# The end of a hybrid retention, state-space and expert block: early operands, a merged order for the two token blocks, and transposes spawned later

## The chip, the cores and the metric

One NeuronCore of one Trainium2 chip runs the whole program, in one launch. The metric is device time in microseconds (us). TensorE (PE) does the matrix products, VectorE (DVE), ScalarE (ACT) and GpSimd (POOL) the elementwise work; SyncE (SP) issues nearly all DMAs, and ACT a few of the stores.

## The reference, cut to what matters

One layer on 256 tokens and 16 meta tokens, model width 2048, all in float32. The parts that the change touches are the last lines of each stage:

```
merged = sigmoid(gate_ret) * y_ret + sigmoid(gate_ssm) * y_ssm
h = h + merged @ w_out                       # residual
xn = rmsnorm(h, norm_ffn_g)
# peer_ffn, here for all 128*128 experts with a sparse gate matrix:
#   u = gelu(xn @ exp_u.T);  Z = gate * u;  y = Z @ exp_v
h = h + y
return rmsnorm(h, norm_final_g)[:, N_META:]  # 256 x 2048
```

## The kernel before, in words

All weights stream from HBM once, as pieces of 128x512. SP loads two pieces at a time (`raw`, 128x1024, four buffers). Each piece is split into a high part `wh` (ACT, L99) and a rest `wl` (DVE, L100), four buffers of each, and TensorE multiplies in three passes: high times high, high times low, low times high.

The order of all work is set by one class, `Stream`. Its `run` goes through the queue of pieces; `now` is the piece's number. For each piece it first splits the piece two places ahead (`self.split(self.now + self.LEAD)`, which also issues the load of the piece six places ahead of that), then calls the piece's hook if it has one, then runs the side work that is due (`due()`), and last the piece's own matmuls. Side work is made of Python generators: `st.spawn(gen, delay, urgent)` puts one on a heap to be resumed `delay` pieces later, and a `yield 1` inside it puts off its next step by one piece. Nothing of this happens on the chip; it only fixes the order in which instructions stand in each engine's queue. Each engine then works through its queue in order and waits on semaphores.

**The merge.** `mixer_out` is called twice; the second call (weights `wso`, `wgs`) makes the merged activations in four column blocks `j` of 512. Products of the kind `product_tok` have the tokens on the partitions: weights are the moving operand, and the matmuls of two pieces are issued together at the odd one, 6 for token block b=0, 6 for b=1 (L234 to L236). When the last piece of a column block is done, `done(b, p)` forms gate times product (DVE, L442), one piece later adds it to `Q.mt` (DVE, L444), and for b=1 spawns `turn(Q.mt, j, merged)`. `turn` transposes the column block in two groups of four 128x128 transposes on TensorE (L463), one piece for ACT to take the result (L469), one for DVE to take the rest (L471), then the second group. `Q.nmerged` counts the finished rows, and the next product (`wout`) asks for them by that count.

**The residual.** The four `wout` products end in `resid(j)`: DVE adds the product to `Q.h2` (L795), and for b=1 a `turn(Q.h2, j, scaled)` is spawned, whose parts are read by the query products `wq` (L206 to L208, 12 matmuls for one piece); the residual is also stored to HBM, to `Q.h2d`.

**The last stage.** Z lies in two tiles: `Q.za`, the first 88 units, on the left side of the on-chip memory, and `Q.zb`, the last 40, on the right. In the V stage, unit `i` of 128 takes four pieces of 128x512; `split_w(i)` makes the high and low part of Z's row block `i` (pool `wp`, two buffers, on the right) two units ahead, and the matmuls (L1063 to L1065) add into eight PSUM tiles `Q.y[q, b]`, column quarter q and token block b. For the last unit the matmuls wait for all four pieces and then run b=0 with q=0..3, and b=1 with q=0..3. `fin_open`, hooked to piece 2 of the last unit, gives back `wp` and `zbp` and opens the pool `fin` in their place; into it SP loads the residual (`Q.h3`, 2 MB, one DMA) and the final norm's weights, spread over the partitions (`Q.gfin`, 1 MB, one DMA). `finish(b)` is called once for each token block: four adds from PSUM on DVE (L1100), four squares with a row sum on ACT (L1101), four products with the weights on POOL (L1102), the sum and the reciprocal root (L1103, then `rsqrt`: DVE L162 and a power on POOL, L163), four scalings on DVE (L1107) and four stores, from SP and ACT in turn (L1108).

Of the kernel before, what the change touches and what calls it, by code (L numbers as in the profile page):

```python
# [8 lines left out]
F32 = mybir.dt.float32  # L9
F32R = mybir.dt.float32r  # L10
U32 = mybir.dt.uint32
AF = mybir.ActivationFunctionType
OP = mybir.AluOpType
AX = mybir.AxisListType
# [3 lines left out]
D = 2048  # L18
# [4 lines left out]
EPS = 1e-6  # L23
# [3 lines left out]
NE = 128  # L27
ZB = 40
# [98 lines left out]
def build(ctx, tc, a):  # L127
    nc = tc.nc
    act, vec, pool, pe = nc.scalar, nc.vector, nc.gpsimd, nc.tensor
# [4 lines left out]
    def opened(name, bufs=1, **kw):  # L134
        g = tc.tile_pool(name=name, bufs=bufs, reuse_waits="tile", **kw)
        setattr(P, name, g.__enter__())
        guards[name] = g
        return getattr(P, name)

    def closed(*names):  # L140
        for n in names:
            guards.pop(n).__exit__(None, None, None)
            delattr(P, n)
# [6 lines left out]
    st = Stream(nc, P.raw, P.part)  # L150
# [7 lines left out]
    Q = Names()  # L158

    def rsqrt(dst, ps, mul, add):  # L160

        vec.tensor_scalar(dst, ps, mul, add, op0=OP.mult, op1=OP.add)  # L162
        pool.tensor_tensor(dst, dst, mhalf.to_broadcast(list(dst.shape)), op=OP.pow)  # L163
# [13 lines left out]
    def rows(dst, c, diag):  # L177

        pool.tensor_tensor(diag.rearrange("p (b t) -> p b t", b=2), ident.unsqueeze(1).to_broadcast([128, 2, 128]),
                           c.unsqueeze(2).to_broadcast([128, 2, 128]), op=OP.mult)  # L180
        yield 3
        pe.matmul(dst, ones, diag, start=True, stop=True)
        yield 1
# [61 lines left out]
    def w_in(done, full, hook=None, early=False):  # L245
        i = wcount[0]
        wcount[0] += 1
        c = slice(0 if full else NM, T)
        if early:
            moving, count = lambda: (Q.x0h[:, :, c], Q.x0l[:, :, c]), None  # L250
        else:
            moving, count = lambda: (Q.xh[:, :, c], Q.xl[:, :, c]), lambda: Q.nx
        product([a["win"][i, 0], a["win"][i, 1]], moving, done, hook, count)
# [168 lines left out]
    def mixer_out(name, gate_name, first, hooks):  # L422

        G = {}

        def gate(j):
            def done(b, p):
                if b == 0:
                    G[j] = P.mwork.tile([128, 2, 512], F32, name="sig")
                act.activation(G[j][:, b], p, AF.Tanh, scale=0.5)  # L430
                return
                yield
            product_tok([a[gate_name][j, i] for i in range(8)], lambda: (Q.xh[:, :, NM:], Q.xl[:, :, NM:]), done,
                        hooks.get(("gate", j)))

        def out(j):
            def done(b, p):
                m, t = Q.mt[:, b, j * 512:j * 512 + 512], G[j][:, b]
                if first:
                    vec.scalar_tensor_tensor(m, t, 1.0, p, op0=OP.add, op1=OP.mult)  # L440
                    return
                vec.scalar_tensor_tensor(t, t, 1.0, p, op0=OP.add, op1=OP.mult)  # L442
                yield 1, 0.7
                vec.tensor_add(m, m, t)  # L444
                if b:
                    st.spawn(turn(Q.mt, j, merged), 1, True)
            product_tok([a[name][j, i] for i in range(16)], lambda: (Q.gh, Q.gl), done, hooks.get(("out", j)),
                        lambda: Q.ngated)

        for j in range(4):  # L450
            gate(j)
            out(j)
            if first and j == 1:
                w_in(dt_done, True)

    def turn(x, j, done):

        for i in range(2):
            f = 4 * j + 2 * i
            ps = P.psm.tile([128, 512], F32, name="mix")  # L460
            for n in range(4):
                c = (f + n // 2) * 128
                pe.transpose(ps[:, n * 128:n * 128 + 128], x[:, n % 2, c:c + 128], ident)  # L463
            yield 1
            yield from done(f, ps)
# [324 lines left out]
    def resid(j):  # L790
        c = slice(j * 512, j * 512 + 512)

        def done(b, p):
            h = Q.h2[:, b, c]
            vec.scalar_tensor_tensor(h, p, 0.5, h, op0=OP.mult, op1=OP.add)  # L795
            if b:
                st.spawn(turn(Q.h2, j, scaled), 1, True)
                if j == 3:
                    st.spawn(norm(), 2, True)
                st.spawn(keep_h2(), 8)  # L800
            yield 1, 0, 0.6
            act.activation(P.h2p.tile([128, 512], F32, name="junk"), h, AF.Square, accum_out=Q.ss[:, b, j:j + 1])

        def keep_h2():
            nc.sync.dma_start(Q.h2d[:, :, c], Q.h2[:, :, c])
            return
            yield

        return done
# [10 lines left out]
    def norm():  # L820
        yield 6
        sq = P.bconst.tile([128, 2], F32, name="sq")
        vec.tensor_reduce(sq, Q.ss, axis=AX.X, op=OP.add)
        Q.rt = P.bconst.tile([128, 2], F32, name="rt")
        rsqrt(Q.rt, sq, 1.0 / D, EPS)
        yield 3
        ps = P.psm.tile([128, 512], F32, name="mix")
        yield from rows(ps[:, :S], Q.rt, P.h2p.tile([128, 512], F32, name="junk")[:, :S])
        act.activation(Q.rb, ps[:, :S], AF.Copy)
        st.spawn(topk(), 1)  # L830
# [236 lines left out]
    def vpiece(i, q):  # L1067
        def f(h, lo):
            if i < NE - 1:
                for b in range(2):  # L1070
                    v_mm(i, q, b, h, lo)
                if q == 3:
                    del Q.w[i]
                    if i + 2 < NE:
                        st.spawn(split_w(i + 2), 0)
            else:
                Q.last.append((h, lo))
                if q == 3:
                    for b in range(2):
                        for qq in range(4):  # L1080
                            v_mm(i, qq, b, *Q.last[qq])
                        finish(b)
        return f

    def fin_open():
        closed("wp", "zbp")
        w = opened("fin", side="right")
        Q.h3 = w.tile([128, 2, 4, 512], F32, name="h3")
        nc.sync.dma_start(Q.h3, Q.h2d.rearrange("p b (q f) -> p b q f", q=4))
        Q.gfin = w.tile([128, 4, 512], F32, name="gfin")  # L1090
        nc.sync.dma_start(Q.gfin, bass.AP(tensor=a["gfin"].tensor, offset=a["gfin"].offset,
                                          ap=[[0, 128], [512, 4], [1, 512]]))

    def finish(b):
        w = P.fin
        pp = w.tile([128, 6], F32, name="pp", bufs=2)
        y = w.tile([128, 4, 512], F32, name="y", bufs=2)
        for q in range(4):
            h = Q.h3[:, b, q]
            vec.tensor_add(y[:, q], Q.y[q, b], h)  # L1100
            act.activation(w.tile([128, 512], F32, name="junk"), y[:, q], AF.Square, accum_out=pp[:, q:q + 1])  # L1101
            pool.tensor_mul(h, y[:, q], Q.gfin[:, q])  # L1102
        vec.tensor_reduce(pp[:, 4:5], pp[:, :4], axis=AX.X, op=OP.add)  # L1103
        rsqrt(pp[:, 5:6], pp[:, 4:5], 1.0 / D, EPS)
        for q in range(4):
            h = Q.h3[:, b, q]
            vec.tensor_scalar(h, h, pp[:, 5:6], None, op0=OP.mult)  # L1107
            (act if q % 2 else nc.sync).dma_start(a["out"][b * 128:b * 128 + 128, q * 512:q * 512 + 512], h)  # L1108


    def ret_open():
# [21 lines left out]
    for j in range(2 * PH):  # L1133
        product([a["wq"][j, 0], a["wq"][j, 1]], lambda: (Q.xgh, Q.xgl), query(j), query_open if j == 1 else None,
                lambda: Q.nxg)
        if j == 1:

            q = st.queue[-8:]
# [2 lines left out]
        product([a["pu"][i, 0], a["pu"][i, 1]], lambda: (Q.xgh, Q.xgl), unit(i), u_open if i == 0 else None)  # L1141
    for i in range(NE):
        for q in range(4):
            hook = {(0, 0): v_open, (0, 3): v_open3, (NE - 1, 2): fin_open}.get((i, q))
            st.queue.append((a["pv"][i, q // 2], vpiece(i, q), hook))

    xnp = opened("xn")
# [5 lines left out]
    w = P.ret  # L1153
# [17 lines left out]
    def square(k):  # L1171
        i = 1 if k % 2 else k % 4
        first = k < 3
        sq = acc[:, i] if first else w.tile([128, T], F32, name="t1") if i == 1 else \
            w.tile([128, T], F32, name="xnf", bufs=3)
        if i == 1:
            pool.tensor_mul(sq, ht[:, k], ht[:, k])
        else:
            act.activation(sq, ht[:, k], AF.Square)
        if not first:  # L1180
            (pool if i == 1 else vec).tensor_add(acc[:, i], acc[:, i], sq)
# [154 lines left out]
```

## Time and profile before

| what | value |
|---|---|
| median of 3 runs (lowest to highest) | 3411.99 us (3411.63 to 3413.03) |
| the profiled execution's own time | 3412.41 us |
| its span, first to last instruction | 3410.5 us |
| mean granted TensorE clock | 0.995 of full speed |
| busy in the span: PE / DVE / ACT / POOL | 3358.5 / 2343.0 / 1738.2 / 648.9 us |
| DMA, mean over the span | 182 GB/s |

The time is measured around the program, so that it is 1.9 us above the span. TensorE is at work for almost the whole span; what another engine does costs time only where TensorE waits for it, or after TensorE's last matmul.

### The profile page before, as it was taken

What the parts mean: (1) busy time and instruction counts of PE and PEld (TensorE: products, weight loads), DVE (VectorE), ACT (ScalarE), POOL (GpSimd) and SP (SyncE); (2) the same over time, 40 slices, a digit from 0 to 9 for tenths busy, and PEclk for the clock granted to TensorE, in tenths of its full rate; (3) what the DMA queues carried; (4) which work ended last, traced back from release to release, by engine and by line L of the source; (5) the groups of instructions that cost most, each with busy time, mean ns of one, the idle gap of its engine ahead of it and who ended that gap; (6) DMA issues with size and microseconds to landing.
All of it is one profiled execution on the core that took longest, in us unless ns stands there. A gap on an engine that the chain in (4) does not pass through costs nothing. (4 is left out here: it accounts for less than half of the span.)

```text
span 3410.5 us, 60879 instructions
## 1 busy us (share of the span) xinstructions
PE 3358.5 (98%) x22616; PEld 3103.3 (91%) x22616; DVE 2343.0 (69%) x4518; ACT 1738.2 (51%) x3132; POOL 648.9 (19%) x743
## 2 busy tenths in 40 slices
PE   9999999999999999999999999999999999999996
PEld 8999999888899999977778999999999988888885
DVE  7555555555578878855556899899999655555554
ACT  5444444444455555544455555555555555555553
POOL 2100110000023223310000111356778100000001
PEclk9999999999999999999999999999999999999998
DMA  5555555566655565555566566555555666666664
GB/s 187 163 167 167 167 167 163 174 197 204 188 175 171 179 189 174 173 173 182 181 206 209 175 188 188 180 175 175 178 175 174 190 193 192 195 193 193 195 193 160
DMA packets 172664, 619.80 MB, mean 182 GB/s; under 512 B 20144, under 2 KB 22064, under 8 KB 171856
## 3 DMA queue, kind: packets, MB, share of 16 engines
q1 hardware_dynamic: 168144, 602.15, 57.4%
q0 software_dynamic: 3648, 12.72, 1.3%
q8 instruction: 178, 2.92, 0.4%
q14 instruction: 118, 0.97, 0.1%
q10 hardware_dynamic: 576, 1.05, 0.1%
HBM read 611.52 MB, written 4.33 MB: 181 GB/s over the span
## 5 line engine op out<-in xcount | busy, mean ns | idle before, releaser
L100 DVE TENSOR_TENSOR wl<-raw,wh 128x512 fp32r<-128x512 f32 x2244 | 1633.9, 732 | 995.4 <-ACT wh L99 776.9
L99 ACT ACTIVATE wh<-raw 128x512 fp32r<-128x512 f32 x2244 | 1409.8, 630 | 1320.0 <-PE acc L207 672.5
L206 PE MATMUL acc<-xh,wh 128*128 128x272 f32 (+1 forms) x2704 | 786.8, 291 | 0.0
L208 PE MATMUL acc<-xh,wl 128*128 128x272 f32 (+1 forms) x2704 | 772.0, 286 | 0.6 <-DVE wl L100 0.6
L207 PE MATMUL acc<-xl,wh 128*128 128x272 f32 (+1 forms) x2704 | 769.7, 285 | 0.0
L208 PE MATMUL acc<-xgh,wl 128*128 128x256 f32 x2304 | 644.8, 280 | 0.0
L206 PE MATMUL acc<-xgh,wh 128*128 128x256 f32 x2304 | 644.3, 280 | 0.0
L207 PE MATMUL acc<-xgl,wh 128*128 128x256 f32 x2304 | 644.2, 280 | 0.0
L206 PEld LDWEIGHTS acc<-xh,wh 128*128 128x128 f32 x2704 | 509.9, 189 | 3.9 <-ACT cth L572 1.2
L207 PEld LDWEIGHTS acc<-xl,wh 128*128 128x128 f32 x2704 | 510.0, 189 | 0.7
L208 PEld LDWEIGHTS acc<-xh,wl 128*128 128x128 f32 x2704 | 509.9, 189 | 0.8 <-DVE wl L100 0.8
L207 PEld LDWEIGHTS acc<-xgl,wh 128*128 128x128 f32 x2304 | 433.2, 188 | 0.0
L206 PEld LDWEIGHTS acc<-xgh,wh 128*128 128x128 f32 x2304 | 432.7, 188 | 0.0
L208 PEld LDWEIGHTS acc<-xgh,wl 128*128 128x128 f32 x2304 | 432.6, 188 | 0.0
L1063 PE MATMUL y<-wh,wzh 128*128 128x512 f32 x1024 | 398.7, 389 | 0.0
L1065 PE MATMUL y<-wh,wzl 128*128 128x512 f32 x1024 | 398.6, 389 | 0.0
L1064 PE MATMUL y<-wl,wzh 128*128 128x512 f32 x1024 | 398.6, 389 | 0.0
L1065 PEld LDWEIGHTS y<-wh,wzl 128*128 128x128 f32 x1024 | 192.3, 188 | 39.9
L1064 PEld LDWEIGHTS y<-wl,wzh 128*128 128x128 f32 x1024 | 192.3, 188 | 39.8
L1063 PEld LDWEIGHTS y<-wh,wzh 128*128 128x128 f32 x1024 | 192.3, 188 | 39.7
L979 POOL TENSOR_SCALAR o<-iota,tp 128x128 fp32r<-128x128 f32 x256 | 220.9, 871 | 22.5 <-PE g L995 18.4
L234 PE MATMUL acc<-wh,gh 128*128 128x512 f32 x512 | 199.8, 390 | 0.0
(315 smaller groups left out, 3764.6 us busy)
## 6 DMA issues: line engine op xcount, KB each, us to landing
raw<-in_win SPq DMA_DIRECT2D x354, 512.0 KB, 3.7
raw<-in_pu SPq DMA_DIRECT2D x256, 512.0 KB, 3.6
raw<-in_pv SPq DMA_DIRECT2D x256, 512.0 KB, 3.6
raw<-in_wro SPq DMA_DIRECT2D x64, 512.0 KB, 4.3
raw<-in_wso SPq DMA_DIRECT2D x64, 512.0 KB, 3.9
raw<-in_wga SPq DMA_DIRECT2D x32, 512.0 KB, 3.7
raw<-in_wgs SPq DMA_DIRECT2D x32, 512.0 KB, 3.6
raw<-in_wout SPq DMA_DIRECT2D x32, 512.0 KB, 4.2
```

The source lines that it names most:

```text
L99: self.nc.scalar.activation(h, r, AF.Copy)
L100: self.nc.vector.tensor_sub(lo, r, h.bitcast(F32))
L206: pe.matmul(p, h[:, s], mh[:, kk], start=kk == 0, stop=False)
L207: pe.matmul(p, h[:, s], ml[:, kk], start=False, stop=False)
L208: pe.matmul(p, lo[:, s], mh[:, kk], start=False, stop=kk == nk - 1)
L234: pe.matmul(p, sh[:, k, t], wh, start=k == 0, stop=False)
L979: pool.tensor_scalar(o[:, 0], Q.iota, Q.i1[:, tt], None, op0=OP.is_equal)
L1063: pe.matmul(y, wh[:, s], h, start=i == 0, stop=False)
L1064: pe.matmul(y, wh[:, s], lo, start=False, stop=False)
L1065: pe.matmul(y, wl[:, s], h, start=False, stop=i == NE - 1)
```

## The change: what it does

Three edits. First, in the merge `turn(Q.mt, j, merged)` is spawned with delay 3 instead of 1. Second, in the residual `turn(Q.h2, j, scaled)` is spawned with delay 2 instead of 1. Third, the last stage: `fin_open` is hooked to the first piece of unit 91 (`NE - ZB + 3`) instead of the last unit's third, gives back `zap` (the left part of Z, whose 88 units are used up by then) instead of `wp` and `zbp`, and opens `fin` there. The loads of residual and weights are cut into eight and four DMAs of 256 KB, one every four pieces. `finish` is called once, after all 24 matmuls of the last unit, and writes the instructions of both token blocks in one order; quarters 0 and 1 go by POOL (times the weights) and ACT (times the row's scale, stored from ACT's queue), quarters 2 and 3 in one DVE instruction with both factors (stored from SP's queue).

```
-                    st.spawn(turn(Q.mt, j, merged), 1, True)
+                    st.spawn(turn(Q.mt, j, merged), 3, True)
...
-                st.spawn(turn(Q.h2, j, scaled), 1, True)
+                st.spawn(turn(Q.h2, j, scaled), 2, True)
...
                         for qq in range(4):
                             v_mm(i, qq, b, *Q.last[qq])
-                        finish(b)
+                    finish()
...
     def fin_open():
-        closed("wp", "zbp")
-        w = opened("fin", side="right")
+        closed("zap")
+        w = opened("fin")
         Q.h3 = w.tile([128, 2, 4, 512], F32, name="h3")
-        nc.sync.dma_start(Q.h3, Q.h2d.rearrange("p b (q f) -> p b q f", q=4))
         Q.gfin = w.tile([128, 4, 512], F32, name="gfin")
-        nc.sync.dma_start(Q.gfin, bass.AP(tensor=a["gfin"].tensor, offset=a["gfin"].offset,
-                                          ap=[[0, 128], [512, 4], [1, 512]]))
+        def fetch():
+            h = Q.h2d.rearrange("p b (q f) -> p b q f", q=4)
+            for b in range(2):
+                for q in range(4):
+                    nc.sync.dma_start(Q.h3[:, b, q], h[:, b, q])
+                    yield 4
+            for q in range(4):
+                nc.sync.dma_start(Q.gfin[:, q], bass.AP(tensor=a["gfin"].tensor, offset=a["gfin"].offset + 512 * q,
+                                                        ap=[[0, 128], [1, 512]]))
+                yield 4
+        st.spawn(fetch(), 4)
...
+        def add(b, q):
+            vec.tensor_add(y[:, b, q], Q.y[q, b], Q.h3[:, b, q])
+        def square(b, q):
+            act.activation(w.tile([128, 512], F32, name="junk"), y[:, b, q], AF.Square, accum_out=pp[:, b, q:q + 1])
+        def gain(b, q):
+            pool.tensor_mul(z[:, b, q], y[:, b, q], Q.gfin[:, q])
+        def norm(b):
+            vec.tensor_reduce(pp[:, b, 4:5], pp[:, b, :4], axis=AX.X, op=OP.add)
+            rsqrt(pp[:, b, 5:6], pp[:, b, 4:5], 1.0 / D, EPS)
+        def store(b, q):
+            (act if q < 2 else nc.sync).dma_start(a["out"][b * 128:b * 128 + 128, q * 512:q * 512 + 512], z[:, b, q])
+        def by_act(b, q):
+            act.activation(z[:, b, q], z[:, b, q], AF.Copy, scale=pp[:, b, 5:6])
+            store(b, q)
+        def by_vec(b, q):
+            vec.scalar_tensor_tensor(z[:, b, q], y[:, b, q], pp[:, b, 5:6], Q.gfin[:, q], op0=OP.mult, op1=OP.mult)
+            store(b, q)
         for q in range(4):
+            add(0, q)
+            square(0, q)
+            if q < 2:
+                gain(0, q)
+        norm(0)
         for q in range(4):
+            add(1, q)
+            square(1, q)
+            if q < 2:
+                gain(1, q)
+                by_act(0, q)
+        by_vec(0, 2)
+        norm(1)
+        by_vec(0, 3)
+        for q in (0, 1):
+            by_act(1, q)
+        for q in (2, 3):
+            by_vec(1, q)
...
-            hook = {(0, 0): v_open, (0, 3): v_open3, (NE - 1, 2): fin_open}.get((i, q))
+            hook = {(0, 0): v_open, (0, 3): v_open3, (NE - ZB + 3, 0): fin_open}.get((i, q))
```

The program decides where these instructions stand. On TensorE, at the end of the first column block of the merge: the rows ahead are the last matmuls of the `wso` product (moving weights, `gh` and `gl` the mixer's output), `mix` with `m_90` is the first group of transposes of `Q.mt`, and `acc` with `xh` is the next product.

```order
 L235 MATMUL acc<-wh,gl 128x512
 L236 MATMUL acc<-wl,gh 128x512
+L234 MATMUL acc<-wh,xh 128x512
+L235 MATMUL acc<-wh,xl 128x512
+L236 MATMUL acc<-wl,xh 128x512
...
 L463 MATMUL mix<-ident,m_90 128x128 x4
 L234 MATMUL acc<-wh,xh 128x512
```

Twelve matmuls (one pair of pieces) of the next product now stand ahead of the transposes; the second group moves back by the same twelve, and the other three column blocks are alike. In the residual, TensorE's order is the same as before for j=0 to 2, where both delays fall between the same two pairs of pieces; for j=3 (`h_19440` is `Q.h2`), where each piece of `wq` has its own matmuls, it changes:

```order
 L235 MATMUL acc<-wh,ml 128x512
 L236 MATMUL acc<-wl,mh 128x512
+L206 MATMUL acc<-xgh,wh 128x256
+L207 MATMUL acc<-xgl,wh 128x256
+L208 MATMUL acc<-xgh,wl 128x256
...
 L463 MATMUL mix<-ident,h_19440 128x128 x4
 L206 MATMUL acc<-xgh,wh 128x256
```

Here, too, twelve matmuls, those of one `wq` piece, now stand ahead of the first transposes. On SP, whose queue loads V's weights (`raw<-in_pv`), the residual and the weights of the norm stand between the loads (the eight rows of `h_37571` and the four of `gfin` follow one another with two loads between them):

```order
+L89 DMA raw<-in_pv 128x1024 x189
+L1095 DMA h_37571<-h2d 128x512
+L89 DMA raw<-in_pv 128x1024 x2
...
+L1098 DMA gfin<-in_gfin 128x512
+L89 DMA raw<-in_pv 128x1024 x2
+L1098 DMA gfin<-in_gfin 128x512
+L89 DMA raw<-in_pv 128x1024 x45
+L1126 DMA out<-z 128x512 x4
```

Before, both stood behind the last of the 256 loads. At the end of the program DVE has these rows now, from the adds of block b=1 on (`y_33188` to `y_33234` are the four PSUM tiles of that block):

```order
+L1113 TENSOR_TENSOR y<-y_33188,h_37571 128x512
+L1113 TENSOR_TENSOR y<-y_33190,h_37571 128x512
+L1113 TENSOR_TENSOR y<-y_33192,h_37571 128x512
+L1113 TENSOR_TENSOR y<-y_33234,h_37571 128x512
+L1133 SCALAR_TENSOR_TENSOR z<-y,pp,gfin 128x512
+L1122 TENSOR_REDUCE pp<-pp 128x1
 L162 TENSOR_SCALAR pp<-pp 128x1
...
+L1133 SCALAR_TENSOR_TENSOR z<-y,pp,gfin 128x512 x3
```

Before, the four scalings of block 0 stood ahead of these adds. And ACT has these:

```order
+L1116 ACTIVATE junk,pp<-y 128x512 x5
+L1129 ACTIVATE z<-z,pp 128x512
+L1126 DMA out<-z 128x512
+L1116 ACTIVATE junk,pp<-y 128x512
+L1129 ACTIVATE z<-z,pp 128x512
+L1126 DMA out<-z 128x512
+L1116 ACTIVATE junk,pp<-y 128x512 x2
+L1129 ACTIVATE z<-z,pp 128x512
+L1126 DMA out<-z 128x512
+L1129 ACTIVATE z<-z,pp 128x512
+L1126 DMA out<-z 128x512
```

Half of the scaling has moved from DVE to ACT, and each of ACT's four stores stands right behind the scaling that it stores.

## Rows read from the trace of the kernel before

**Rows 1.** The page: the span, and busy time by engine.

```profile
span 3410.5 us, 60879 instructions
PE 3358.5 (98%) x22616; PEld 3103.3 (91%) x22616; DVE 2343.0 (69%) x4518; ACT 1738.2 (51%) x3132; POOL 648.9 (19%) x743
```

**Rows 2.** Timeline of the end: start, length, engine, line, what, [idle before <-releaser].

```profile
3375.44 0.69 DVE L100 TENSOR_TENSOR wl<-raw,wh 128x512 fp32r<-128x512 f32 x1 [0.67 <-ACT wh L99]
...
3379.79 0.39 PE L1065 MATMUL y<-wh,wzl 128*128 128x512 f32 x1
...
3388.39 2.48 DVE L1100 TENSOR_TENSOR y<-y,h 128x512 f32<-128x512 f32 x4 [12.26 <-DMA h<-h2d]
3389.11 0.63 ACT L1101 ACTIVATE junk<-y 128x512 f32<-128x512 f32 x1 [13.71 <-DVE y L1100]
...
3391.91 0.19 ACT L1101 ACTIVATION_READ_ACCUMULATOR junk<-y 128x1 f32 x1
...
3392.32 0.15 DVE L162 TENSOR_SCALAR pp<-pp 128x1 f32<-128x1 f32 x1
```

**Rows 3.** Chain that ended last, from 3379 on: start, length, what.

```profile
3380.66 10.07 DMA gfin<-in_gfin
3390.99 4.93 POOL h L1102 x4
```

**Rows 4.** Waits of TensorE, 1480 to 1960: us in total, times, longest.

```profile
PE mix L463 <- DVE m L444: 7.1, 7, 2.1
PE mix L463 <- DVE h L795: 2.7, 4, 0.7
PE mix L463 <- issue: 2.0, 1, 2.0
```

**Rows 5.** Timelines of TensorE and DVE at the merge's first column block.

```profile
1522.46 0.39 PE L236 MATMUL acc<-wl,gh 128*128 128x512 f32 x1
1524.92 0.30 PE L463 MATMUL mix<-ident,m 128*128 128x128 f32 x1 [2.08 <-DVE m L444]
1525.43 0.55 PE L463 MATMUL mix<-ident,m 128*128 128x128 f32 x3 [0.21 <-DVE m L444]
1525.73 0.48 PE L234 MATMUL acc<-wh,xh 128*128 128x512 f32 x1
...
1524.09 1.29 DVE L444 TENSOR_TENSOR m<-m,sig 128x512 f32<-128x512 f32 x2
```

**Rows 6.** Stretches between both groups, j=0, 1, 2: busy, PEclk, DMA share, GB/s.

```profile
1525.73:1530.17 4.44, 4.44 (x16) 3.43 (x15) 0.93 (x2) 1.18 (x3) 0.00 (x0) 0.62 0.39 122
1596.67:1599.58 2.91, 2.91 (x16) 2.30 (x15) 0.32 (x2) 0.74 (x2) 0.00 (x0) 1.00 0.49 155
1666.01:1670.43 4.42, 4.42 (x15) 3.44 (x14) 0.64 (x2) 1.05 (x3) 0.00 (x0) 0.61 0.38 119
```

**Rows 7.** Timeline of TensorE at the residual's last block.

```profile
1831.12 0.55 PE L463 MATMUL mix<-ident,h 128*128 128x128 f32 x3 [0.68 <-DVE h L795]
```

**Rows 8.** V stage, 3000 to 3370: share of the DMA engines; us to landing.

```profile
q1 hardware_dynamic: 19539, 71.13, 63.4%
...
raw<-in_pv SPq DMA_DIRECT2D x135, 512.0 KB, 4.3
```

**Rows 9.** DVE reading Z's left part: ns, then first and last start.

```profile
L1045 DVE TENSOR_TENSOR wzl<-za,wzh x86: 418/419/421, 2690.7 to 3153.1; 128x256 fp32r<-128x256 f32 x86
```

**Rows 10.** The power on POOL, alone and beside a split; ACT's stores (ns).

```profile
L163 POOL TENSOR_TENSOR pp<-pp,mhalf x2: 572/575/578, 3395.9 to 3403.7; 128x1 f32<-128x1 f32 x2
...
1842.16 0.17 DVE L162 TENSOR_SCALAR rt<-sq 128x2 f32<-128x2 f32 x1
1842.34 0.69 DVE L100 TENSOR_TENSOR wl<-raw,wh 128x512 fp32r<-128x512 f32 x1
1842.47 1.11 POOL L163 TENSOR_TENSOR rt<-rt,mhalf 128x2 f32<-128x2 f32 x1 [357.43 <-DVE rt L162]
...
L1108 ACTq DMA_DIRECT2D out<-h x4: 338/339/374, 3397.4 to 3406.1; - x4
```

More of the change, by code (lines that the diff above doesn't have):

```diff
@@ L1094, in finish @@
-    def finish(b):
-        w = P.fin
-        pp = w.tile([128, 6], F32, name="pp", bufs=2)
-        y = w.tile([128, 4, 512], F32, name="y", bufs=2)
-        for q in range(4):
[L1099 to L1104, printed above, removed]
-        for q in range(4):
-            h = Q.h3[:, b, q]
-            vec.tensor_scalar(h, h, pp[:, 5:6], None, op0=OP.mult)
-            (act if q % 2 else nc.sync).dma_start(a["out"][b * 128:b * 128 + 128, q * 512:q * 512 + 512], h)
+        def fetch():
[8 more added lines that the diff above has]
+                yield 4
@@ new lines, in fin_open, with finish @@
+        st.spawn(fetch(), 4)
+    def finish():
+        w = P.fin
+        pp = w.tile([128, 2, 6], F32, name="pp")
+        y = w.tile([128, 2, 4, 512], F32, name="y")
+        z = w.tile([128, 2, 4, 512], F32, name="z")
+        def add(b, q):
[15 more added lines that the diff above has]
+            store(b, q)
+        for q in range(4):
+            add(0, q)
[3 more added lines that the diff above has]
+        norm(0)
+        for q in range(4):
+            add(1, q)
[10 more added lines that the diff above has]
+            by_vec(1, q)
```

## The prediction

> **What bounds the kernel now.** I start at the page's busy times: TensorE is busy for 3358.5 of 3410.5 us, the next engine, DVE, for 2343.0 [rows 1]. So 52 us are not TensorE's, and the question for each edit is which of these it touches. The timeline of the end gives most of them. TensorE's last matmul starts at 3379.79 and ends at 3380.18 [rows 2]; the span ends at 3410.5, so 30.3 us follow in which TensorE has nothing to do. DVE's idle time ahead of its first add there is 12.26 us, released by the load of the residual. The chain of waits names the other load, that of the norm's weights, 10.07 us, and then four POOL products, 4.93 us [rows 3]. TensorE's waits give the next piece: it waited 7.1 + 2.0 us for the merge's transposes (the 2.0 is one block, booked on no releaser) and 2.7 us for the residual's [rows 4]. What is left, about 10 us, is the start of the program and is not touched.
>
> **Edit 1: the merge's transposes, three pieces later.** At the end of a column block the last `wso` matmul starts at 1522.46, the first transpose waits 2.08 us and the second 0.21 us for DVE's add, and the next product starts at 1525.73 [rows 5], 3.27 us after that matmul. Without a wait that would be one matmul, 0.24 us (a pair of pieces, twelve matmuls, in the 2.91 us of the middle row of [rows 6]), and four transposes, 0.40 us (three take from 1525.43 to 1525.73). So 2.63 us are lost, and the waits of the list (9.1 us in all for four blocks, 2.3 each) say that all four blocks lose alike: 10.5 us. A second loss stands behind it. Between the two groups of transposes lie the same twelve matmuls each time, but they took 2.91 us for j=1 at a granted clock of 1.00, and 4.44 us and 4.42 us for j=0 and j=2 [rows 6], at a mean of 0.62 and 0.61: after TensorE's 2.3 us of waiting the clock stood for most of these stretches at 1.2 GHz instead of 2.4. That is 1.5 us twice, 3.0 us.
>
> After the change twelve matmuls stand ahead of the transposes. DVE's two adds run from 1524.09 to 1525.38 [rows 5], and nothing ahead of them in DVE's queue moves. TensorE would be through the last `wso` matmul at about 1522.7 and through the pair at 1522.7 + 2.72 = 1525.4 (2.72 us is four pieces in 5.44 us, see edit 3, halved). So the adds are ready just as TensorE arrives: the wait goes to nothing, with 0.1 us or so in doubt for each block. The pair itself needs its split weights, which were made ahead of the merge's adds, and its two PSUM buffers, of which the second comes free when DVE has read it in L442. That and one split (0.69) stand ahead of the adds, so it is done before 1523.5, and the pair's second half begins at 1522.7 + 1.36 = 1524.06. What is late next? The group's results are read by ACT and DVE two pieces later than now, and `wout` asks for the last rows at its pieces 13 and 15, where the new order has made them at pieces 5 and 7; that has room. The second group goes back by the same pair and finds its data there, as it does now. Edit 1 is worth 13.5 us; its bounds are 0 (the wait only moves) and 14.
>
> **Edit 2: the residual's transposes, one piece later.** For j=0 to 2 TensorE's order does not change, so that those waits of 0.7 us stay, and only ACT's and DVE's follow-up shifts by a piece, which nothing waits for until `wq`. For j=3 the twelve matmuls of a `wq` piece, some 1.4 us, now cover the wait of 0.68 us [rows 7]. The price would be at the other end: the last rows of `xgl` are now written right ahead of `wq`'s sixth piece instead of one piece earlier. No row shows that order. Between the transposes and these rows stand two ACT and two DVE instructions of the group and two splits (0.63 on ACT, 0.69 on DVE), about 3 us in line, and TensorE has the last two of the three pieces between, 2.8 us, and half a piece more, 0.7, since the rows are used in the piece's second half. So it is likely hidden, by little; at worst a piece, 1.4 us, is lost. I take 0.7 us of gain, between 0.7 lost and 0.9 gained.
>
> **Edit 3: the last stage.** First the loads. Each of Z's row blocks takes (3153.1 - 2690.7)/85 = 5.44 us, and the left part is last read at 3153.1 [rows 9]; the new hook comes some five units later, near 3180, so that SP's queue does not stop at the first load. Twelve loads of 256 KB in the following 65 us add a quarter to a stream that keeps the DMA engines 63.4% busy [rows 8]: 79%. A load of weights lands in 4.3 us and is issued six pieces, 8.2 us, ahead of its split; a 256 KB load in between costs it well under the 3.9 us of slack. So the 12.26 us of waiting disappear, and the cover is the V stage.
>
> Now the new end, step by step, from rows of the old one. Block 0's last matmul is twelve matmuls ahead of the end, near 3377.5, and DVE's last split ends at 3376.13 [rows 2]. Four adds at 0.60 each (2.48 for four) follow from there, limited by the split rather than by PSUM. ACT's first square starts 0.72 after its add, at 3376.85, and four squares take 2.99 (3389.11 to 3392.10), to 3379.84. The sum and the scale's first half take 0.37 after that (3392.10 to 3392.47) [rows 2], to 3380.21. Only then do block 1's adds start, since they stand behind on DVE; their PSUM is ready at 3380.18. ACT starts block 1's first square at 3380.21 + 0.05 + 0.72 = 3380.98. From here ACT is the bound: four squares at 0.75, and two scalings with their stores ahead of the last two squares. A scaling is an ACT instruction of the same size, 0.63, a store holds ACT's queue for 0.34 [rows 10], and I add 0.11 for the two hand-overs: 1.08 twice. That ends at 3380.98 + 2.99 + 2.16 = 3386.13. Sum and scale: 0.37, to 3386.50. The power on POOL starts 0.14 later (1842.33 to 1842.47 in the other norm).
>
> Its length is the one doubt. In the old end it took 0.575 us with DVE idle; in the residual's norm, where DVE began a 128x512 instruction with two operands in on-chip memory just ahead of it, it took 1.11 [rows 10]. In the new order such an instruction, block 0's last scaling on DVE, stands right behind the sum. I take 1.11: to 3387.75. By 0.575 it would be 0.54 us less. The Trainium skill, page "SBUF — State Buffer", section "SBUF: two separate sides", speaks against the order chosen here: VectorE and GpSimd share a pair of ports that one instruction holds to its end, and a VectorE instruction with two inputs in SBUF keeps out a GpSimd one that reads there. By that rule the power waits out the scaling; the row of 1.11 us agrees with it, and without the rule the sum would be 0.54 us better.
>
> Then two scalings on ACT: 0.04 + 1.08 + 0.63 + 0.06, and the last store is issued at 3389.56. DVE's two are done by 3387.8 + 1.4 = 3389.2, ahead of that. From the last store's issue to the end of the span it is 3410.5 - 3406.1 = 4.4 us [rows 10], so the span ends at 3393.96: 13.8 us after TensorE, instead of 30.3. Edit 3 gives 16.5 us. Bounds: 17.5 with the shorter power and no hand-overs, 13 if each of ACT's stores held it a microsecond longer.
>
> **Sum.** 16.5 + 10.5 + 3.0 + 0.7 = 30.7 us. The profiled execution took 3412.4; 3381.7. The median of the runs is 0.4 lower: 3381.3 us, 0.9% faster.
>
> **Rivals.**
> The merge's wait only moves. The margin of edit 1 is nil by the numbers above: adds at 1525.38, TensorE at 1525.4. If DVE's adds come later, because a split that now stands behind them has gone ahead, TensorE waits behind the pair instead, and at 2 us of waiting the clock may drop again. Against it: what stands ahead of the adds does not change. With all of edit 1 lost: 3381.3 + 13.5 = 3394.8.
> The added loads reach the weights. With nothing beside them the 3 MB were there 10.07 us after the second issue [rows 3]; if all of that displaced weights that TensorE waits for, the time is 3381.3 + 10.1 = 3391.4. Against it: 79% busy. A smaller form: at the merge's end the residual's 2 MB load now meets a TensorE that is 2.6 us earlier; should it wait for weights there, these 2.6 us are the most it gives back, 3383.9.
> The end is worth less: ACT, which alternates between squares, scalings and stores, needs 3 us more than summed: 3384.3.
> Slower: SP's queue stops. If the early loads waited for a tile still in use, every load of V's weights behind them would stop too, and TensorE would run dry after 8.2 us. Held for 39 us it would undo the 30.7; held for 50 it would give 3381.3 + 50 - 8.2 = 3423.1. Against it: the left part's last read is some 27 us ahead of the hook.
> That the change does nothing: only if the loads still ended the program; they are issued 130 us ahead of the end.
>
> **How the numbers follow.** All three edits as summed, 3377 to 3388, which takes in the short end: 0.78. The merge's wait moves, wholly or by half, 3388 to 3396: 0.11. Loads collide, 3384 to 3394: 0.06. More gain than summed, since matmuls behind a wait also ran slightly apart: 0.03. SP stops: 0.02. The range from 3377 to 3390 leaves out about 0.15. A measurement of this kernel can tell 0.2%, 6.8 us, from no change; every case but the last is beyond that, most of them by far. Faster 0.97, same 0.015, slower 0.015.
>
> **What would show it.** Right: in the merge no wait for `m` above 0.3 us, and granted clock 1.00 in the four stretches; in the residual the wait for `h` three times instead of four; in V no idle time of TensorE with loads of `h` and `gfin` among the weights; after TensorE's last matmul 13 to 15 us, with ACT's second block of squares and its stores in the chain of waits, and the second power near 1.1 us. Wrong: waits for `m` above 1 us behind the pair, or TensorE waiting for a split in V or in `wq`.

## The result

| | before | after |
|---|---|---|
| median of the runs | 3412.51 us (3411.63 to 3413.39, 4 runs) | 3380.66 us (3380.47 to 3381.0, 4 runs) |
| ratio of after to before | | 0.9906, 95% interval 0.9894 to 0.9919 |
| the profiled execution's own time, its span | 3412.41, 3410.5 us | 3381.0, 3379.1 us |

The kernel is 31.9 us faster, 0.9%; 3381.3 us was predicted. The page after, busy time by engine, answers to [rows 1]:

```profile
span 3379.1 us, 60883 instructions
PE 3352.3 (99%) x22616; PEld 3100.1 (92%) x22616; DVE 2342.3 (69%) x4514; ACT 1739.6 (51%) x3136; POOL 644.5 (19%) x739
```

The same 22616 matmuls; TensorE's part of the span that is not busy went from 52.0 to 26.8 us. Its busy time fell too, by 6.2 us: 4.4 of these lie between the merge's first and fourth block, 3.0 of them matmuls that no longer run at the lower clock, and 1.4 in the program's first 40 us, where the change does nothing.

The timeline of the end after (start, length, engine, line, what, [idle before <-releaser]), which answers to [rows 2] and [rows 3]:

```profile
3360.80 0.69 DVE L100 TENSOR_TENSOR wl<-raw,wh 128x512 fp32r<-128x512 f32 x1 [0.67 <-ACT wh L99]
3361.41 2.48 DVE L1113 TENSOR_TENSOR y<-y,h 128x512 f32<-128x512 f32 x4
...
3365.15 0.39 PE L1065 MATMUL y<-wh,wzl 128*128 128x512 f32 x1
3365.15 0.16 DVE L1122 TENSOR_REDUCE pp<-pp 128x1 f32<-128x4 f32 x1 [1.26 <-ACT junk L1116]
...
3366.19 0.63 ACT L1116 ACTIVATE junk<-y 128x512 f32<-128x512 f32 x1 [1.07 <-DVE y L1113]
...
3367.81 1.41 DVE L1133 SCALAR_TENSOR_TENSOR z<-y,pp,gfin 128x512 f32<-128x512 f32 x1
...
3371.25 0.16 DVE L1122 TENSOR_REDUCE pp<-pp 128x1 f32<-128x4 f32 x1 [2.03 <-ACT junk L1116]
3371.44 0.15 DVE L162 TENSOR_SCALAR pp<-pp 128x1 f32<-128x1 f32 x1
3371.51 0.74 DVE L1133 SCALAR_TENSOR_TENSOR z<-y,pp,gfin 128x512 f32<-128x512 f32 x1
3371.68 1.00 POOL L163 TENSOR_TENSOR pp<-pp,mhalf 128x1 f32<-128x1 f32 x1 [3.00 <-DVE pp L162]
3372.70 0.72 ACT L1129 ACTIVATE z<-z,pp 128x512 f32<-128x512 f32 x1 [1.49 <-POOL pp L163]
...
3373.87 0.72 ACT L1129 ACTIVATE z<-z,pp 128x512 f32<-128x512 f32 x1 [0.45 <-ACT z L1129]
3374.62 0.34 ACTq L1126 DMA_DIRECT2D out<-z  x1
```

The first add follows the last split of weights without a gap, 4.1 us ahead of TensorE's end at 3365.54; no load is waited for. The long stretch from 3366.19 to 3371.25 is ACT's: four squares and two scalings with their stores. Then the chain goes DVE, POOL, ACT, to the issue of the last store at 3374.62. 13.6 us follow TensorE's last matmul.

TensorE's waits in the merge and the residual (1480 to 1960) are down to one row, where [rows 4] had three:

```profile
PE mix L463 <- DVE h L795: 2.0, 3, 0.7
```

and in the merge's first column block (timeline; see [rows 5]) TensorE goes from matmul to transposes and on without waiting:

```profile
1524.86 0.39 PE L236 MATMUL acc<-wl,xh 128*128 128x512 f32 x1
1525.09 0.60 PE L463 MATMUL mix<-ident,m 128*128 128x128 f32 x4
1525.44 0.48 PE L234 MATMUL acc<-wh,xh 128*128 128x512 f32 x1
...
1523.72 1.28 DVE L444 TENSOR_TENSOR m<-m,sig 128x512 f32<-128x512 f32 x2
```

DVE's adds end at 1525.00, 0.09 us ahead of the transposes, as close as the sum had it. The stretch behind the transposes (columns as in [rows 6]) has the full clock:

```profile
1525.44:1528.27 2.83, 2.83 (x15) 2.30 (x14) 1.42 (x4) 0.96 (x3) 0.00 (x0) 1.00 0.54 152
```

For all kernels that follow the span is cut at the same places of TensorE's timeline: the start of the last `wso` matmul of the merge's first and fourth column block, the start of the last `wout` matmul, of the first key product of the queries (L857), and of V's first matmul, and the end of the last one. The fourth block's own wait lies in the column "to wout's end".

| kernel | span | first to fourth merge block | to wout's end | to the first key product | V | after TensorE |
|---|---|---|---|---|---|---|
| before | 3410.5 | 211.20 | 96.29 | 15.72 | 696.51 | 30.32 |
| after | 3379.1 | 199.97 | 93.58 | 15.25 | 696.51 | 13.56 |
| end alone | 3395.0 | 211.09 | 97.89 | 15.72 | 696.52 | 13.54 |
| merge alone | 3395.9 | 199.96 | 93.62 | 15.72 | 696.52 | 30.28 |
| residual alone | 3411.3 | 211.20 | 96.29 | 15.24 | 696.51 | 30.34 |
| early loads, old order | 3381.4 | 199.96 | 93.60 | 15.25 | 696.52 | 16.33 |
| new order, late loads | 3392.3 | 199.97 | 93.61 | 15.25 | 696.51 | 26.20 |
| scaling ahead of the norm | 3378.2 | 199.97 | 93.60 | 15.25 | 696.52 | 13.09 |
| loads at once | 3380.4 | 199.96 | 93.61 | 15.24 | 697.39 | 13.65 |
| residual later still | 3376.1 | 199.96 | 90.94 | 15.24 | 696.52 | 13.56 |
| end dealt out anew | 3377.8 | 199.97 | 93.61 | 15.24 | 696.51 | 12.36 |
| both of these | 3374.8 | 199.97 | 90.93 | 15.25 | 696.52 | 12.32 |
| the change once more | 3378.6 | 199.97 | 93.60 | 15.25 | 696.52 | 13.54 |

The stretch from the program's start to the first of these places is in no column. It differs by up to 1.8 us between kernels that are alike there (1521.59 to 1523.43 us), so that the columns tell more than the spans. One run of the residual alone took 4144.8 us at a mean granted clock of 0.75; it is left out of the times given for that kernel.

### The profile page after: what moved, and what is told of

It is laid out like the page before. It is cut to its first block, busy times and chain, and to the rows that moved or that the text cites. A ratio compares the mean times of both kernels' runs of the same rounds, so it can differ in the third digit from the quotient of the medians.

```text
span 3379.1 us, 60883 instructions
## 1 busy us (share of the span) xinstructions
PE 3352.3 (99%) x22616; PEld 3100.1 (92%) x22616; DVE 2342.3 (69%) x4514; ACT 1739.6 (51%) x3136; POOL 644.5 (19%) x739
## 4 chain that ended last, share of the span: by engine, by line
PE 56%; ACT 0%; DVE 0%; issue 0%; POOL 0%; POOLq 0%; ACTq 0%
PE acc L208 8%; PE acc L207 8%; PE acc L206 8%; PE y L1065 7%; PE y L1064 7%; PE y L1063 7%; PE acc L234 3%; PE acc L235 3%; PE acc L236 3%; PE g L995 1%; PE mix L463 0%; PE mix L857 0%; DVE wl L100 0%; ACT junk L1116 0%; ACT wh L99 0%
```

## The experiments

### The three edits apart

The end alone takes both spawn delays back:

```
-                    st.spawn(turn(Q.mt, j, merged), 3, True)
+                    st.spawn(turn(Q.mt, j, merged), 1, True)
...
-                st.spawn(turn(Q.h2, j, scaled), 2, True)
+                st.spawn(turn(Q.h2, j, scaled), 1, True)
```

> Only the last stage is changed; both spawn delays are 1 as before. By the theory that the three edits act apart: TensorE keeps its 2.1 us waits at the four column blocks of the merge and its two stretches at the lower clock, TensorE ends near 3380 as before, 13.6 us follow it instead of 30.3; 16.5 to 17 us faster than before, about 3395.6. By the rival that part of the end's gain comes from the merge (TensorE reaching V earlier shifts what the loads collide with): clearly less than 16 us.

Measured: 3396.84 us against 3412.45 in the same runs, ratio 0.9954 (0.9941 to 0.9968). That is 15.6 us, a microsecond short of what was expected. The table shows that the end itself is worth all of it (30.32 to 13.54) and that the missing piece of the profiled execution is in the column "to wout's end", 97.89 instead of 96.29, far from the edit. The 20 us from the fourth merge block on (columns as in [rows 6]), first in the kernel before, then in this one:

```profile
1733.00:1753.00 20.00, 17.71 (x82) 14.27 (x81) 11.61 (x18) 8.33 (x14) 0.00 (x0) 1.00 0.76 265
```

```profile
1733.00:1753.00 20.00, 17.71 (x75) 14.04 (x74) 10.54 (x17) 8.29 (x14) 0.00 (x0) 0.91 0.73 248
```

TensorE waits equally long in both (17.71 of 20 us busy, 2.29 lost), but here the clock fell behind the fourth block's wait too, where it had stayed at 1.00 in the run of before, and this cost 1.6 us. So how many of the four blocks pay is not the same in each execution: two of four in the profile of before, three here, two again with the residual alone (mean clock 0.91, 1.00, 0.91 and 1.00 in the 20 us from each block on).

The merge alone is the kernel before with this:

```
-                    st.spawn(turn(Q.mt, j, merged), 1, True)
+                    st.spawn(turn(Q.mt, j, merged), 3, True)
```

> Only the merge's transposes are spawned with delay 3. Theory: the four waits of 2.1 + 0.2 us go (10.5 us) and with them the two stretches at 1.2 GHz (3.0 us): 13.5 us faster than before, about 3399.0, granted clock 1.00 behind all four blocks. Rival, that the clock falls on its own and not after the wait: 10.5 us, 3402, with stretches below 1.00 left in the merge.

3398.06 us against 3412.45, ratio 0.9959 (0.9946 to 0.9973): 14.4 us. The columns say 11.24 us from the first to the fourth block and 2.67 us for the fourth, 13.9 us. The 20 us from each of the four blocks on have neither idle time nor a granted clock below 1.00 any more:

```profile
1522.00:1542.00 20.00, 20.00 (x92) 16.37 (x91) 12.43 (x19) 9.32 (x17) 0.00 (x0) 1.00 0.56 182
1588.60:1608.60 20.00, 20.00 (x92) 16.31 (x91) 12.42 (x19) 9.27 (x17) 0.00 (x0) 1.00 0.56 181
1655.20:1675.20 20.00, 20.00 (x93) 16.27 (x92) 12.42 (x19) 9.26 (x17) 0.00 (x0) 1.00 0.59 183
1721.90:1741.90 20.00, 20.00 (x93) 16.51 (x93) 12.39 (x19) 9.59 (x17) 0.00 (x0) 1.00 0.83 289
```

The rival, that the clock falls by itself, would have left some of these stretches below 1.00, and 3.0 us; it is out. In none of the ten profiles with the merge's transposes moved did the clock fall in the merge; in all three with the waits it did.

The residual alone is the kernel before with this:

```
-                st.spawn(turn(Q.h2, j, scaled), 1, True)
+                st.spawn(turn(Q.h2, j, scaled), 2, True)
```

> Only the residual's transposes are spawned with delay 2. Theory: three of the four 0.7 us waits stay, the fourth goes; 0.7 us less span than before, a difference that the times can hardly tell from none. Rival, that the later rows of xgl make wq's sixth piece wait: a wait of TensorE on xgl there and no gain or a loss up to 0.7 us.

3412.57 us against 3412.45, ratio 1.0 (0.999 to 1.0009): the times do not tell it from no change, as expected. The column does: 15.72 to 15.24, 0.48 us. The wait for `h` occurs three times instead of four, and none on `xgl` came.

By their times the three edits apart give 29.9 us, 2.0 less than the whole change. Of these, 1.6 us is the third fall of the clock in the profile of the end alone; by the columns they add up.

### The end: loads or order?

Here the loads are early, as in the change, and the old `finish(b)` is called for each token block:

```
                             v_mm(i, qq, b, *Q.last[qq])
-                    finish()
+                        finish(b)
...
```

> All of the change, but the end in the old order: finish is called for each token block, with POOL's four products and DVE's four scalings. Theory by rows of before: with the data there, block 0's part runs beside TensorE's last twelve matmuls from 3376.1 on the old clock; POOL's four products end about 5 us after the first add and hold up the power; block 1's adds wait behind block 0's scalings; the old 22 us from first add to end then start some 8 us earlier relative to TensorE's end than with the load's 8.2 us wait: 22.1 - 4.1 = 18 us after TensorE, some 4.5 us more than with the new order, about 3385. So 12 us of the end's 16.7 would be the loads and 4.5 the order. Rival, that the loads are nearly all: within 1 us of the whole change; rival, that the order is half: 3389.

3383.60 us, ratio 0.9916 (0.9902 to 0.9929); 16.33 us after TensorE, where 18 were expected. So with the old order the early loads are worth 14.0 of the end's 16.8 us, and the new order the other 2.8. The expectation was 1.7 us off, and the timeline of this run says where:

```profile
3360.94 2.48 DVE L1110 TENSOR_TENSOR y<-y,h 128x512 f32<-128x512 f32 x4
...
3361.85 5.05 POOL L1112 TENSOR_TENSOR h<-y,gfin 128x512 f32<-128x512 f32 x4 [691.26 <-DVE y L1110]
...
3364.87 0.15 DVE L162 TENSOR_SCALAR pp<-pp 128x1 f32<-128x1 f32 x1
3366.86 0.58 POOL L163 TENSOR_TENSOR pp<-pp,mhalf 128x1 f32<-128x1 f32 x1
```

POOL's first product starts 0.9 us after the first add; before it started 2.6 us after it, at 3390.99 [rows 3], since it waited for the norm's weights, which landed behind the residual. The 22 us of the old order had this wait in them. What is left of the old order's weakness can be seen as well: the power is ready to go at 3365.02 and POOL is at its products until 3366.9.

The other way round: the loads stay late, in the place of `wp` and `zbp`, and the order is the new one (the sums are written over the residual, since that place is small):

```
     def fin_open():
-        closed("zap")
-        w = opened("fin")
+        closed("wp", "zbp")
+        w = opened("fin", side="right")
...
-        y = w.tile([128, 2, 4, 512], F32, name="y")
+        y = Q.h3
```

> The whole change, but residual and norm weights are loaded where the kernel before loads them, by two DMAs behind TensorE's end into the place of wp and zbp; the sums are written over the residual, since the place is small. The order of the end is the new one. Theory: the new order needs 17.7 us from its first add to the end, the first add waits 8.2 us for the residual behind TensorE, so 25.9 us behind TensorE's last matmul instead of 13.6, and the order alone is worth 30.3 - 25.9 = 4.4 us, more than the 2.8 it is worth with early loads. Rival, that the loads' 10 us hold the new order up as much as the old one: near 30 us.

3393.85 us, ratio 0.9945 (0.9928 to 0.9961); 26.20 us after TensorE, 25.9 expected. The wait is the old one, and what follows is the new order's 18 us:

```profile
3374.35 2.48 DVE L1103 TENSOR_TENSOR h<-y,h 128x512 f32<-128x512 f32 x4 [12.29 <-DMA h<-h2d]
...
3376.91 2.49 POOL L1109 TENSOR_TENSOR z<-h,gfin 128x512 f32<-128x512 f32 x2 [705.29 <-DVE h L1103]
```

The order is worth 4.1 us with late loads and 2.8 us with early ones; the early loads are worth 12.6 us with the new order and 14.0 with the old one. POOL is late again for its first product, 2.6 us after the first add, but in the new order only two products stand ahead of the power, not four.

### Must the loads be spread?

```
-        def fetch():
-            ...
-        st.spawn(fetch(), 4)
+        nc.sync.dma_start(Q.h3, Q.h2d.rearrange("p b (q f) -> p b q f", q=4))
+        nc.sync.dma_start(Q.gfin, bass.AP(tensor=a["gfin"].tensor, offset=a["gfin"].offset,
+                                          ap=[[0, 128], [512, 4], [1, 512]]))
```

> The whole change, but at the early hook residual and weights are loaded by one DMA of 2 MB and one of 1 MB as before, instead of twelve of 256 KB. Theory that the spreading matters: with 3 MB in the queue a load of V's weights behind it lands some 7 to 10 us later, more than the 3.9 us of slack, so TensorE waits once or twice near 3175 for 3 to 6 us in all, perhaps with a stretch at the lower clock. Rival, that V hides it anyway: no wait of TensorE in V and the time of the whole change.

3381.99 us, ratio 0.9906 (0.989 to 0.9923), not to be told from the change's. The expected 3 to 6 us did not come. ACT's waits between 3150 and 3200 have one row that the change's do not have, one load that came late, and TensorE's wait that follows from it, in V:

```profile
ACT wh L99 <- DMA raw<-in_pv: 4.2, 1, 4.2
```

```profile
PE y L1064 <- DVE wl L100: 0.2, 1, 0.2
```

V took 697.39 instead of 696.51 us, 0.9 us more, of which the list has 0.2. The rest stands at the same place, in the rows of TensorE and ACT behind the late load:

```profile
3177.81 0.39 PE L1065 MATMUL y<-wh,wzl 128*128 128x512 f32 x1
3178.28 0.49 PE L1063 MATMUL y<-wh,wzh 128*128 128x512 f32 x1
3179.01 0.50 PE L1064 MATMUL y<-wl,wzh 128*128 128x512 f32 x1 [0.23 <-DVE wl L100]
3179.34 0.40 PE L1065 MATMUL y<-wh,wzl 128*128 128x512 f32 x1
...
3177.60 0.63 ACT L99 ACTIVATE wh<-raw 128x512 fp32r<-128x512 f32 x1 [4.17 <-DMA raw<-in_pv]
```

The three matmuls from 3178.28 on follow the one ahead of them by 0.47, 0.73 and 0.33 us, where it is 0.23 in the rows around; only part of that shows as idle time. ACT was idle for 4.2 us ahead of its split, 3.5 more than in the longest of its other waits there (0.7), and 0.9 of these reached TensorE. The expectation counted only the slack of the load (3.9 us). The 2.6 us that did not reach TensorE are about the 2.7 us of the two pieces that are split ahead of their matmuls: an estimate from these rows, not tested by itself. The rival was right but for this 0.9 us. With the twelve loads spread, V shows no wait at all.

### The power beside a scaling

```
         by_vec(0, 2)
-        norm(1)
         by_vec(0, 3)
+        norm(1)
```

> The whole change, with block 0's last scaling on DVE put ahead of block 1's norm instead of right behind it; nothing else moves, and DVE had 2.0 us idle there. Theory of the shared port pair: the second power no longer runs beside an instruction with two operands in on-chip memory and takes 0.58 us instead of 1.00; the span is 0.4 us shorter. Rival, that the 1.00 us is POOL's own after a longer idle time (3.0 us idle ahead of it here, 0.7 ahead of the first): it stays near 1.0 and nothing is gained.

13.09 us after TensorE instead of 13.56, and 3380.19 us (ratio 0.9903, 0.9886 to 0.9919). The timeline of this run:

```profile
3371.01 0.15 DVE L162 TENSOR_SCALAR pp<-pp 128x1 f32<-128x1 f32 x1
3371.24 0.56 POOL L163 TENSOR_TENSOR pp<-pp,mhalf 128x1 f32<-128x1 f32 x1 [3.00 <-DVE pp L162]
...
3371.84 1.42 DVE L1133 SCALAR_TENSOR_TENSOR z<-y,pp,gfin 128x512 f32<-128x512 f32 x2 [0.67 <-POOL pp L163]
```

The same instruction after the same 3.00 us of idle time takes 0.56 us with DVE idle and 1.00 us beside DVE's scaling of two operands in on-chip memory. So it is the neighbour, not POOL's idle time. The Trainium skill, page "SBUF — State Buffer", section "SBUF: two separate sides", has this as a port pair that VectorE and GpSimd hold in turn, and these two runs agree with it. DVE pays as well: a scaling takes 0.71 us with POOL idle (two in 1.42 in the last row) and 1.41 us where it meets POOL's second product (3367.81 in the change's timeline); ACT's squares are later there, so that this costs nothing. In both meetings the instruction that began first kept its time: the scaling at 3371.51, 0.17 us ahead of the power, took 0.74 us, and POOL's two products took 2.49 us.

### Two improvements

The change leaves three waits of 0.7 us in the residual, since a delay of 2 puts the transposes between the same matmuls as 1 does. One piece more moves them behind a pair; for j=3 the queries need the rows, and it keeps 2:

```
-                st.spawn(turn(Q.h2, j, scaled), 2, True)
+                st.spawn(turn(Q.h2, j, scaled), 3 if j < 3 else 2, True)
```

> The whole change, and the residual's transposes for j=0 to 2 with delay 3 (j=3 keeps 2). Theory: now these three groups, too, stand behind a pair of matmuls, and the last three waits of 0.7 us go; 2.5 us less span than the whole change. Rival, that the adds' wait only shows up elsewhere (ACT's squares or the splits late): less than 1 us.

The column "to wout's end" goes from 93.58 to 90.94, 2.6 us; the waits for `h` are gone. 3377.79 us, ratio 0.9895 (0.9879 to 0.9912).

In the end ACT's queue is the long stretch. Here its squares of block 1 stand without scalings in between, and DVE takes one quarter more (which it stores from SP):

```
-            (act if q < 2 else nc.sync).dma_start(...)
+            (act if q < b + 1 else nc.sync).dma_start(...)
...
         for q in range(4):
             add(0, q)
             square(0, q)
-            if q < 2:
-                gain(0, q)
+        gain(0, 0)
         norm(0)
         for q in range(4):
             add(1, q)
             square(1, q)
             if q < 2:
                 gain(1, q)
-                by_act(0, q)
+        by_act(0, 0)
         by_vec(0, 2)
-        norm(1)
         by_vec(0, 3)
+        norm(1)
...
+        by_vec(0, 1)
```

> The whole change with the end's work dealt out anew: ACT does block 1's four squares without scalings in between, then three scalings; DVE does five, two of them ahead of block 1's norm and none beside the power; POOL three products. Theory that ACT's queue bounds the end from block 1's first square on: the norm comes when DVE is through its two scalings, some 1.4 us earlier, the power takes 0.6, and the last store is issued 1.6 us earlier than with the whole change. Rival, that POOL's products and DVE's scalings, which meet now, hold each other up: no gain.

12.36 us after TensorE instead of 13.56, 3379.27 us, ratio 0.99 (0.9883 to 0.9916). The timeline:

```profile
3367.70 2.07 DVE L1133 SCALAR_TENSOR_TENSOR z<-y,pp,gfin 128x512 f32<-128x512 f32 x2
...
3369.69 0.14 DVE L1122 TENSOR_REDUCE pp<-pp 128x1 f32<-128x4 f32 x1
...
3370.10 0.56 POOL L163 TENSOR_TENSOR pp<-pp,mhalf 128x1 f32<-128x1 f32 x1 [1.54 <-DVE pp L162]
...
3372.62 0.34 ACTq L1126 DMA_DIRECT2D out<-z  x1
```

Now the norm waits for DVE, whose two scalings took 2.07 us beside POOL's products, against 1.42 with POOL idle. The last ACT store is issued 11.3 us after the first add (3361.31) instead of 13.2, 1.9 us earlier; but what follows TensorE got only 1.2 us shorter. The last store is now one of SP's five, issued at 3372.8 (stores: ns, then first and last start):

```profile
L1126 SPq DMA_DIRECT2D out<-z x5: 332/343/396, 3369.1 to 3372.8; - x5
```

From there to the end it is 5.0 us, where it was 4.5. Both theories had a part of it: ACT was the bound, and DVE beside POOL took some of the gain back.

Both together, beside the unaltered change:

> The whole change with both improvements that the earlier runs measured: the residual's first three groups of transposes with delay 3, and the end's work dealt out anew. If they act apart, as their places 1500 us from each other suggest: 2.7 us less in the residual and 1.2 us less behind TensorE's last matmul, 3.9 us less than the whole change in the same runs.

> The whole change once more, unaltered, as the measure for the runs beside it: 0.906 to 0.991 of before is read as 0.9906 plus or minus the interval, about 3380.7, and 13.6 us behind TensorE's last matmul.

3377.01 us for both, 3381.05 us for the change, 3412.57 us for the kernel before in these runs; ratios to before 0.9896 (0.9879 to 0.9912) and 0.9908 (0.9891 to 0.9924). They add up: 4.0 us faster than the change, 2.7 us in the residual and 1.2 us behind TensorE. This version beats both kernels.

## Why the prediction was right, point by point

**Edit 1**, predicted 13.5 us: 13.9 measured, 11.2 up to the fourth block and 2.7 for it. Waits and clock belong together: where the wait goes, the lower clock goes with it, and where it stays, the clock falls behind two or three of the four blocks. What failed to be seen is that this number is not fixed; the 3.0 us taken for the clock hold for the profiled execution. The waits themselves gave 10.9 us instead of 10.5; where the other 0.4 comes from was not traced.

**Edit 2**, predicted 0.7 us: 0.48. The wait is gone, and the feared one on `xgl` did not come. TensorE's busy time between the two places went from 15.04 to 15.25 us; why was not traced.

**Edit 3**, predicted 16.5 us: 16.8. Step by step, counted from TensorE's end: first add 4.05 us ahead, measured 4.13; block 1's first square at 0.80, measured 0.65; second norm's sum at 5.95, measured 5.71; the power 1.11, measured 1.00; a scaling and its store 1.08, measured 1.17 (the scaling 0.72 instead of 0.63); the last store's issue at 9.38, measured 9.08; from there to the end 4.4, measured 4.5. The errors are at most 0.3 us and partly cancel. That ACT bounds the stretch and that the second power runs beside a scaling was as summed. The row of 1.11 us was that of a power over two columns, while the one at the end has one. Powers over two columns stand elsewhere in the trace of before (ns, shortest, median and longest):

```profile
L163 POOL TENSOR_TENSOR ncol<-ncol,mhalf x16: 706/714/1108, 90.9 to 1476.9; 128x2 f32<-128x2 f32 x16
```

So the neighbour costs 0.40 us over two columns (0.71 to 1.11) and 0.44 over one (0.56 to 1.00). The prediction set 0.575 against 1.11 and so counted the columns as part of the neighbour's price, for 0.11 us too much.

The sum of the columns, 13.9 + 0.5 + 16.8 = 31.2, is 0.2 short of the spans' 31.4: 0.4 us less ahead of the merge and 0.1 more between the queries and V, where the change does nothing.

That the predicted time came within 0.6 us is in part luck. By the medians the gain is 31.9 us, 1.2 more than the 30.7 of the sum, but the median of before, from which the prediction subtracted, rose by 0.5 us with its fourth run.

Of the rivals, the merge's wait did not move; the added loads cost TensorE nothing, and even all at once only 0.9 us; SP's queue did not stop. In its timeline the first early load (`h`) follows the load ahead of it (the last of seven, ended at 3168.74) by 0.1 us:

```profile
3152.09 16.65 SPq L89 DMA_DIRECT2D raw<-in_pv  x7
3168.83 0.38 SPq L1095 DMA_DIRECT2D h<-h2d  x1
3171.21 2.97 SPq L89 DMA_DIRECT2D raw<-in_pv  x2
```

Two expectations had a term wrong: that of the old order with early loads, the loads' share of the end (14.0 instead of 12 us), for want of the wait of POOL for the norm's weights; and that of the loads at once, TensorE's loss (0.9 instead of 3 to 6 us), since it counted the load's slack alone.

## What to carry to other kernels

A transpose that waits for the last adds of a product costs TensorE the wait and possibly a stretch at the lower clock as well; one pair of the next product's matmuls ahead of it hid both here, and a delay in the generator's units only helps if it crosses a place where matmuls are issued. Operands of a last stage belong in a place that comes free early, under the long stage ahead of it: that was 12.6 to 14.0 of the 16.8 us, and the finer order of instructions only the rest. Keep instructions of DVE with two operands in on-chip memory away from a POOL instruction that others wait for; here one such meeting cost 0.44 us.

## What the runs showed of the hardware that was not expected

The clock fell behind two of four equal waits of 2.3 us in two executions, behind three of four in another, and in the merge of none of the ten without these waits. A load of V's weights for which ACT waited 4.2 us made V 0.9 us longer, with a listed wait of TensorE of only 0.2 us. Where a scaling on DVE and an instruction of POOL met, the one that began later took 0.4 to 0.7 us longer. ACT's scaling by a column of factors took 0.71 us, where its plain copies and squares of the same size take 0.63.
